# A transformer layer step with padded weight rows and padded token tiles

## The chip, the cores and the metric

The kernel runs on one core of a Trainium2 chip. The metric is the device time of one execution in microseconds (us); lower is better. A profile of one execution is at hand beside the times of three runs.

## The reference, cut to what matters

One layer of a decoder for 256 prompt tokens and 8 sample tokens, 264 tokens in all, with a model width of 2048. Everything is float32. Each line with `@` is a large weight matrix:

```
z  = rmsnorm(x) @ w_in                    # 2048 x 5128
x += concat(rg_lru(z), mlstm(z)) @ w_out  # recurrences of the two head groups
k, v = rmsnorm(mem) @ w_k, rmsnorm(mem) @ w_v    # 256 memory tokens
q  = rmsnorm(x) @ w_q
x += softmax(q k^T / sqrt(512)) v @ w_o   # 4 heads; samples use cached k, v
h  = silu(rmsnorm(x) @ w_gate) * (rmsnorm(x) @ w_up)   # 2048 -> 5632
x += h @ w_down
y  = rmsnorm(x)
```

## The kernel before

Tokens lie transposed: the 2048 features in 16 chunks of 128 partitions, the 264 tokens along the free dimension. A product with a weight matrix goes by *steps*: a step makes 128 output features for all tokens, from one piece of the weights of 128 partitions x 2048 columns (16 blocks of 128 x 128, 1 MB). There are 257 steps (16 of them, those of V, turn the operands round: the memory tokens are stationary and 512 columns of weights stream). The list `steps` holds them in order; the loop at line 1234 goes through it.

To keep float32's precision at the fast rate of the type float32r, each operand is split in two parts of float32r, high and low. `mm3` (line 179) multiplies one block by one chunk of tokens with three matmuls into the same bank: weights high by tokens high, high by low, low by high. Each of these matmuls comes with a load of its weight block (PEld in the profile), which runs while the matmul before it streams its tokens.

**Weights.** `load_piece` (line 142) issues a piece's DMA from SP's queue into one of 3 raw buffers of 2048 columns. SP's queue runs in the order in which it is written, two to three pieces ahead. `split_half` (line 150) splits a piece by halves of 1024 columns (8 blocks), one step ahead of the matmuls: ScalarE (ACT) copies the raw values to float32r in `wh`, VectorE (DVE) subtracts that from the raw ones into `wl`. Each of `wh` and `wl` has 4 buffers of 1024 columns, so two steps of two halves. `W` (line 169) gives a block's two parts to `mm3`. `split_gates` (line 506) does the same for the one step of the gates, whose 8 used columns allow both parts in one block.

**Tokens.** `Arr` (line 110) is an array of chunks, 4 chunks of 264 columns in one tile of the tag `B`, which has 26 slots; `HL` (line 124) is a pair of such arrays for high and low. The tag `B` serves everything else of that size too. A slot goes to the tile that asks next, so which slot a tile has follows from the order in which the program asks.

SBUF is laid out in the order in which tags are first asked for: the constants, then the tags `raw`, `B`, `wh`, `wl`, `t` and the smaller ones. Every tile begins at a multiple of 32 bytes.

**Start.** Lines 1211 to 1223 write out by hand the first loads on SP's queue: tokens in groups, the first piece in quarters among them, then pieces 1 and 2 with the third and fourth group of tokens. The first piece's halves are split in 4 and in 2 parts.

Other work (recurrences, norms, attention, the sample tokens' caches by GpSimd's queue) is put between the steps by `pump`, as far as the planned clocks of VectorE and ScalarE leave room.

Of the kernel before, what the change touches and what calls it, by code (L numbers as in the profile page):

```python
# [10 lines left out]
F32 = mybir.dt.float32  # L11
F32R = mybir.dt.float32r
I32 = mybir.dt.int32
AF = mybir.ActivationFunctionType
# [3 lines left out]
P = 128  # L18
# [4 lines left out]
N = T + NS  # L23
# [57 lines left out]
def layer_kernel(ctx: ExitStack, tc, xT, memT, vec, wrg, w_in, w_out, w_q, w_k, w_v, w_o,  # L81
# [3 lines left out]
    act, dve, pe = Engine(nc.scalar, price_act), Engine(nc.vector, price_dve), Engine(nc.tensor, price_pe)  # L85
    pool_e, sp = nc.gpsimd, nc.sync

    const = ctx.enter_context(tc.tile_pool(name="const", bufs=1))
    sb = ctx.enter_context(tc.tile_pool(name="sb", bufs=1))
# [2 lines left out]
    ctx.enter_context(tc.manual_schedule(engines={mybir.EngineType.SP}))  # L92

    uid = [0]

    def nm(s):
        uid[0] += 1
        return f"{s}_{uid[0]}"

    def B(shape, dt=F32):  # L100
        return sb.tile(shape, dt, tag="B", bufs=NB, name=nm("B"))

    def tmp(w=N, tag="t"):
        t = sb.tile([P, N], F32, tag=tag, bufs=NT if tag == "t" else NL, name=nm(tag))
        return t[:, :w]

    def ltmp(w=N):
        return tmp(w, "lt")

    class Arr:  # L110


# [2 lines left out]

        def tile(self, q):
            if q not in self.t:
                self.t[q] = B([P, min(4, self.nb), self.w], self.dt)
            return self.t[q]

        def __call__(self, c):
            return self.tile(c // 4)[:, c % 4, :]
# [14 lines left out]
    steps = []  # L137
    LD, LS = 3, 1

    raws, splits = {}, {}  # L140

    def load_piece(i):
        if i >= len(steps) or i in raws:
            return
        src, cols = steps[i][0], steps[i][1]
        r = sb.tile([P, 2048], F32, tag="raw", bufs=3, name=nm("raw"))
        sp.dma_start(r[:, :cols], src)
        raws[i] = r

    def split_half(i, h, parts=1):  # L150
        if i >= len(steps):
            return
        if steps[i][2] is pe_if:
            if h == 0:
                split_gates(i)
            return
        cols = steps[i][1]
        lo, hi = h * 1024, min(cols, (h + 1) * 1024)
        wh = sb.tile([P, 1024], F32R, tag="wh", bufs=4, name=nm("wh"))
        wl = sb.tile([P, 1024], F32R, tag="wl", bufs=4, name=nm("wl"))  # L160
        r = raws[i]
        n = (hi - lo) // parts
        with tc.high_priority():
            for o in range(0, hi - lo, n):
                st["split"] = act.activation(wh[:, o: o + n], r[:, lo + o: lo + o + n], AF.Copy)
                dve.tensor_sub(wl[:, o: o + n], r[:, lo + o: lo + o + n], wh[:, o: o + n])
        splits[i, h] = (wh, wl)

    class W:
        def __init__(self, i):  # L170
            self.i = i

        def __call__(self, c, w=P):
            per = 1024 // w
            wh, wl = splits[self.i, c // per]
            o = (c % per) * w
            return wh[:, o: o + w], wl[:, o: o + w]

    def mm3(ps, a, b, start, stop):
        ah, al = a  # L180
        bh, bl = b
        pe.matmul(ps, ah, bh, start=start, stop=False)
        pe.matmul(ps, ah, bl, start=False, stop=False)
        pe.matmul(ps, al, bh, start=False, stop=stop)

    st = {}
# [18 lines left out]
    def side(g, prio=0):  # L205
        x = Gen(g, prio)
        gens.append(x)
        gens.sort(key=lambda q: q.prio)
        return x
# [25 lines left out]
    def bank(tag="mm"):  # L235
        return psm.tile([P, 512], F32, tag=tag, bufs=4, name=nm(tag))

    warm_act = const.tile([P, 1], F32, name="warm_act")
    act.activation(warm_act, ones[:, 0:1], AF.Square)

    def warm(n, w=None):
# [263 lines left out]

    def split_gates(i):

        r = raws[i]
        for h in range(2):
            w = sb.tile([P, 8, P], F32R, tag="wh", bufs=4, name=nm("wh"))  # L510
            x = r[:, h * 1024: h * 1024 + 1024].rearrange("p (c m) -> p c m", m=P)
            with tc.high_priority():
                act.activation(w[:, :, 0:64], x[:, :, 0:64], AF.Copy)
                dve.tensor_sub(w[:, :, 64:128], x[:, :, 0:64], w[:, :, 0:64].bitcast(F32))
            splits[i, h] = w
# [303 lines left out]
    def proj(src, rhs, evac, cols=2048, n=N, need=()):  # L819

        def f(i):
            ps = bank()
            w = W(i)
            nch = cols // P
            for c in range(nch):
                mm3(ps[:, :n], w(c), rhs(c), c == 0, c == nch - 1)
            return ps
        steps.append((src, cols, f, evac, need))
# [191 lines left out]
    def evac_k(h, j):  # L1020
        def f(ps):
            if j == 0:
                kv["k", h] = HL(4, T)
            t = tmp(T)
            act.activation(t, ps[:, :T], AF.Copy)
            pool_e.dma_start(o_k[:, 4 * h + j, :], t)
            kh, kl = kv["k", h](j)
            act.activation(kh, ps[:, :T], AF.Copy)
            dve.tensor_sub(kl, ps[:, :T], kh.bitcast(F32))
            if j == 3:  # L1030
                st["att", h] = side(attend(h), 1)
        return f

    def pe_v(h, k4):
        def f(i):
            if k4 == 0:
                kv["vps"] = [bank(), bank()]
            w = W(i)
            for c in range(4):
                kc = k4 * 4 + c  # L1040
                mh, ml_ = rm(kc)
                wh, wl = w(c, 512)
                for tb in range(2):
                    ps = kv["vps"][tb]
                    s = slice(tb * P, tb * P + P)
                    pe.matmul(ps, mh[:, s], wh, start=(kc == 0), stop=False)
                    pe.matmul(ps, mh[:, s], wl, start=False, stop=False)
                    pe.matmul(ps, ml_[:, s], wh, start=False, stop=(kc == KC - 1))
            return kv["vps"]
        return f  # L1050

    def evac_vm(h):
        def f(vps):
            vv = B([P, 2, 512], F32R), B([P, 2, 512], F32R)
            kv["v", h] = vv
            vf = B([P, 2, 512])
            for tb in range(2):
                vh = vv[0][:, tb, :]
                act.activation(vh, vps[tb], AF.Copy)
                dve.tensor_sub(vv[1][:, tb, :], vps[tb], vh.bitcast(F32))  # L1060
                act.activation(vf[:, tb, :], vps[tb], AF.Copy)
                pool_e.dma_start(o_v[tb * P: tb * P + P, h * 512: h * 512 + 512], vf[:, tb, :])
            kv["vn"] = h + 1
        return f
# [57 lines left out]
    for h in range(H):  # L1122
        for j in range(4):
            proj(w_k[4 * h + j], rm, evac_k(h, j), n=T, need=("memg",))
        for k4 in range(4):
            steps.append((w_v[h, k4], 2048, pe_v(h, k4), evac_vm(h) if k4 == 3 else None, ()))

    def ro(c):
        return st["o"](c)
# [81 lines left out]
    def load_x(lo, hi):  # L1211
        sp.dma_start(xres[:, lo:hi, :], xT[:, lo:hi, :])

    r = sb.tile([P, 2048], F32, tag="raw", bufs=3, name=nm("raw"))
    raws[0] = r
    for h in range(4):
        if h < 2:
            load_x(2 * h, 2 * h + 2)
        sp.dma_start(r[:, h * 512: h * 512 + 512], w_in[0][:, h * 512: h * 512 + 512])
    for q in range(1, 4):  # L1220
        load_x(4 * q, 4 * q + 4)
        if q < 3:
            load_piece(q)

    with tc.high_priority():
        for c in range(KC):
            split(*xn(c), xres[:, c, :], V("g_mix", c))
            if c == 1:
                split_half(0, 0, 4)
            elif c == 3:  # L1230
                split_half(0, 1, 2)

    pend = []
    for i, (src, cols, pef, evf, need) in enumerate(steps):
        load_piece(i + LD - 1)
        if i == 5:
            finish(lambda: fn.done)
# [9 lines left out]
        now = pe.clock  # L1247
        dve.clock, act.clock = max(dve.clock, now), max(act.clock, now)
        split_half(i + LS, 0)
        if i + LS < len(steps) and steps[i + LS][1] > 1024:  # L1250
            split_half(i + LS, 1)
# [7 lines left out]
        if evf is not None:  # L1259
            pend.append((evf, ps))  # L1260
        load_piece(i + LD)
        pump(pe.clock + SLACK)
        if i == 24:
# [5 lines left out]
    for lo, hi in ((0, 1), (1, 2), (2, 4), (4, 6), (6, 8), (8, 10), (10, 12), (12, 14), (14, 16)):  # L1269
        for c in range(lo, hi):  # L1270
            e, r = (pool_e, rstd) if c in POOLC else (dve, fin["ps"][:, :N])
# [108 lines left out]
```

## Time and profile before

| | |
|---|---|
| median of 3 runs | 1575.6 us (1570.88 to 1576.71) |
| the profiled execution | 1576.51 us |
| its span, from the first to the last instruction | 1574.8 us |
| TensorE busy (PE) | 1556.5 us, 99% |
| VectorE (DVE), ScalarE (ACT) busy | 1051.4 us, 789.7 us |
| moved by DMA | 325.97 MB, mean 207 GB/s |
| mean granted TensorE clock | 0.991 |

In the profile, PE is TensorE's matmuls and PEld its weight loads; `mm<-B,wh` is a matmul into a bank `mm` from a token tile `B` and a weight tile `wh`. L60 is the line of a helper that issues every instruction of ACT, DVE and PE, so groups are told apart by tiles. "128x264" is partitions by columns of the streamed operand. A row of the timeline has its start in us, its length in us, the engine and the instruction; neighbours that are alike are merged (x2).

### The profile page before, as it was taken

Reading aid. Unit: us, or ns where it says so; the run is one execution under the profiler, and the core shown is the slowest. Engines: PE = TensorE matmul, PEld = TensorE weight load, DVE = VectorE, ACT = ScalarE, POOL = GpSimd, SP = SyncE. Lnnn points to the kernel's source line nnn. Section 1 sums busy time; section 2 is a strip of 40 time slices with the busy share of each in tenths; the row PEclk is TensorE's granted clock in tenths of the full one; section 3 lists DMA queues with packets and bytes.
Section 4 is the critical chain, followed back from the end, with each engine's and each line's share of the span. In section 5 each row is a group of like instructions: output and inputs, shape, how many; then the busy total and the mean of one; then the engine's idle time right before and its main releaser. Section 6 shows DMA issues by size and latency. Waiting matters only on the chain.

```text
span 1574.8 us, 29829 instructions
## 1 busy us (share of the span) xinstructions
PE 1556.5 (99%) x12340; PEld 1532.6 (97%) x12340; DVE 1051.4 (67%) x2021; ACT 789.7 (50%) x1252; POOL 109.6 (7%) x174
## 2 busy tenths in 40 slices
PE   9999999999999999999999999999999999999997
PEld 8999999999999889999999999999999999999997
DVE  7876877787699899956655555455555554555554
ACT  7465675565455656645444444333444433344463
POOL 0001210000124333200000000000000000000000
PEclk9999999999999999999999999999999999999998
DMA  8455875546689788745545555555455554555452
GB/s 304 161 174 172 294 269 205 178 145 245 248 321 346 302 305 319 251 161 178 187 164 185 188 180 175 181 188 186 174 179 186 187 181 172 184 188 184 156 179 99
DMA packets 55303, 325.97 MB, mean 207 GB/s; under 512 B 6688, under 2 KB 7120, under 8 KB 24448
## 3 DMA queue, kind: packets, MB, share of 16 engines
q1 hardware_dynamic: 39744, 270.68, 48.4%
q0 software_dynamic: 15136, 53.16, 9.4%
q8 instruction: 96, 1.57, 0.4%
q14 instruction: 39, 0.32, 0.1%
q10 hardware_dynamic: 288, 0.23, 0.1%
HBM read 312.78 MB, written 11.28 MB: 206 GB/s over the span
## 4 chain that ended last, share of the span: by engine, by line
PE 94%; DMA 2%; DVE 2%; ACT 1%; issue 1%; DVEq 0%; POOL 0%; SPq 0%; ACTq 0%
PE mm L60 89%; PE ax L60 4%; DVE B L60 1%; DMA o_sc<-B 1%; ACT B L60 1%; DMA raw<-w_in 1%; ACT wh L60 0%; DMA B<-scr 0%; DVE wl L60 0%; ACT L60 0%; DMA vecs<-vec 0%; DMA scr<-lt 0%; DVE t L60 0%; DVE dw L60 0%; ACT t L60 0%
## 5 line engine op out<-in xcount | busy, mean ns | idle before, releaser
L60 PE MATMUL mm<-B,wh 128*128 128x264 f32 (+1 forms) x7520 | 1379.0, 285 | 4.8 <-DVE B L60 3.0
L60 PEld LDWEIGHTS mm<-B,wh 128*128 128x128 f32 x7520 | 1168.4, 189 | 6.4 <-ACT cso L60 3.1
L60 PE MATMUL mm<-B,wl 128*128 128x264 f32 (+1 forms) x3744 | 1062.8, 284 | 0.6 <-DVE wl L60 0.6
L60 ACT ACTIVATE wh<-raw 128x1024 fp32r<-128x1024 f32 (+2 forms) x518 | 536.9, 1038 | 692.0 <-PE mm L60 574.6
L60 DVE TENSOR_TENSOR wl<-raw,wh 128x1024 fp32r<-128x1024 f32 (+2 forms) x516 | 619.0, 1201 | 356.7 <-ACT wh L60 350.0
L60 PEld LDWEIGHTS mm<-B,wl 128*128 128x128 f32 x3744 | 706.7, 189 | 1.1 <-DVE wl L60 1.0
L60 DVE TENSOR_TENSOR t<-mm,rstd 128x264 f32<-128x264 f32 x104 | 44.9, 432 | 60.2 <-PE mm L60 60.2
L60 PE MATMUL mm<-wh,B 128*128 128x512 f32 x256 | 82.3, 395 | 0.0
L60 DVE TENSOR_TENSOR xres<-xres,mm 128x264 f32<-128x264 f32 x80 | 34.2, 428 | 47.1 <-PE mm L60 47.1
L1272 POOL TENSOR_TENSOR B<-B,rstd 128x264 f32<-128x264 f32 x4 | 2.8, 743 | 864.9 <-ACT rstd L60 864.9
L60 PEld LDWEIGHTS mm<-wh,B 128*128 128x128 f32 x256 | 47.8, 189 | 9.8
L60 DVE SCALAR_TENSOR_TENSOR B<-B,dw 128x256 f32<-128x256 f32 x128 | 52.6, 465 | 2.3 <-ACT dw L60 2.3
L60 PE MATMUL mm<-wl,B 128*128 128x512 f32 x128 | 50.6, 395 | 0.0
L60 DVE SCALAR_TENSOR_TENSOR dw<-B,qsm,dw 128x256 f32<-128x256 f32 x96 | 47.9, 500 | 1.4 <-ACT dw L60 0.7
L60 PE MATMUL ax<-B,B 128*128 128x256 f32 (+3 forms) x288 | 48.2, 308 | 0.3 <-DVE B L60 0.3
L60 PEld LDWEIGHTS ax<-B,B 128*128 128x128 f32 x288 | 40.8, 189 | 4.0 <-issue 1.2
L977 POOL TENSOR_TENSOR ds<-dw,ds 128x256 fp32r<-128x256 f32 x32 | 35.4, 1107 | 115.3 <-ACT ds L60 115.2
L60 ACT ACTIVATE B<-xres,vecs 128x264 fp32r<-128x264 f32 (+1 forms) x64 | 31.1, 503 | 2.5 <-DMA xres<-xT 1.4
L60 ACT ACTIVATE t<-xres 128x264 f32<-128x264 f32 x60 | 23.9, 413 | 15.4 <-DVE xres L60 15.4
L60 PEld LDWEIGHTS mm<-wl,B 128*128 128x128 f32 x128 | 24.1, 188 | 5.0
L966 POOL DMA_DIRECT2D B<-kcT x32 | 17.5, 546 | 147.4 <-DVE B L60 127.0
L60 DVE TENSOR_TENSOR acc_x<-acc_x,t 128x264 f32<-128x264 f32 x59 | 25.2, 428 | 0.9 <-ACT t L60 0.5
(157 smaller groups left out, 740.0 us busy)
## 6 DMA issues: line engine op xcount, KB each, us to landing
raw<-w_gu SPq DMA_DIRECT2D x88, 1024.0 KB, 4.8
raw<-w_in SPq DMA_DIRECT2D x40, 1024.0 KB, 4.9
raw<-w_d SPq DMA_DIRECT2D x32, 1024.0 KB, 4.8
raw<-w_out SPq DMA_DIRECT2D x16, 1024.0 KB, 4.8
B<-kcT POOLq DMA_DIRECT2D x32, 512.0 KB, 6.1
raw<-w_q SPq DMA_DIRECT2D x16, 1024.0 KB, 5.0
B<-vcT POOLq DMA_DIRECT2D x32, 512.0 KB, 7.2
raw<-w_k SPq DMA_DIRECT2D x16, 1024.0 KB, 6.4
```

The source lines that it names most:

```text
L60: return f(*a, **k)
L966: pool_e.dma_start(kc, kcT[h, b])
L977: pool_e.tensor_sub(ws[:, 1], acc, ws[:, 0].bitcast(F32))
L1272: e.tensor_mul(st["y"](c), st["y"](c), r)
```

## The change

Five things change together; no arithmetic does.

- Every token tile of the tag `B` has 4 x 264 + 32 = 1088 columns. In arrays of 264 columns, tiles of odd number begin 32 columns (128 bytes) into theirs; others begin at 0.
- The two parts of a half piece share one tile `w` of 8 x 264 + 64 = 2176 columns, of which there are 4. From column 48 on it has 8 rows of 264 columns, one for each block: 128 columns of the high part and, right behind them, 128 of the low part; 8 columns are left unused. The gates' step uses the same rows.
- The steps of K and V (`wide`) keep contiguous parts: high in columns 0 to 1023 and low in 1056 to 2079 of such a tile.
- The raw buffers are halves of 1024 columns, 5 of them in place of 3 of 2048, and each piece is loaded by two DMAs, the first piece's quarters into its two halves.
- A small tile `pad` of 16 columns is the first in its pool, and the constant `warm_act` becomes a column of it. That takes 32 bytes from the constants and puts 64 ahead of `raw`, so that `raw`, `B` and `w` begin on a multiple of 256 bytes.

```diff
+    pad = sb.tile([P, 16], F32, tag="pad", bufs=1, name="pad")
...
+    BW = 4 * N + 32
+    WO, WW = 48, 8 * N + 64
...
         def tile(self, q):
             if q not in self.t:
-                self.t[q] = B([P, min(4, self.nb), self.w], self.dt)
+                t, o = B([P, BW], self.dt), 32 * (q % 2) if self.w == N else 0
+                self.t[q] = t[:, o: o + 4 * self.w].rearrange("p (c n) -> p c n", n=self.w)
             return self.t[q]
...
         src, cols = steps[i][0], steps[i][1]
-        r = sb.tile([P, 2048], F32, tag="raw", bufs=3, name=nm("raw"))
-        sp.dma_start(r[:, :cols], src)
-        raws[i] = r
+        raws[i] = []
+        for o in range(0, cols, 1024):
+            r = raw_half()
+            w = min(1024, cols - o)
+            sp.dma_start(r[:, :w], src[:, o: o + w])
+            raws[i].append(r)
+
+    def raw_half():
+        return sb.tile([P, 1024], F32, tag="raw", bufs=5, name=nm("raw"))
...
-        cols = steps[i][1]
-        lo, hi = h * 1024, min(cols, (h + 1) * 1024)
-        wh = sb.tile([P, 1024], F32R, tag="wh", bufs=4, name=nm("wh"))
-        wl = sb.tile([P, 1024], F32R, tag="wl", bufs=4, name=nm("wl"))
-        r = raws[i]
-        n = (hi - lo) // parts
+        nch = min(8, steps[i][1] // P - 8 * h)
+        w = sb.tile([P, WW], F32R, tag="w", bufs=4, name=nm("w"))
+        if i in wide:
+            wh, wl = w[:, 0: 1024], w[:, 1056: 2080]
+            with tc.high_priority():
+                act.activation(wh, raws[i][h], AF.Copy)
+                dve.tensor_sub(wl, raws[i][h], wh.bitcast(F32))
+            splits[i, h] = (wh, wl)
+            return
+        wh, wl = wrows(w, i)
+        r = raws[i][h].rearrange("p (c m) -> p c m", m=P)
+        n = nch // parts
         with tc.high_priority():
-            for o in range(0, hi - lo, n):
-                st["split"] = act.activation(wh[:, o: o + n], r[:, lo + o: lo + o + n], AF.Copy)
-                dve.tensor_sub(wl[:, o: o + n], r[:, lo + o: lo + o + n], wh[:, o: o + n])
+            for o in range(0, nch, n):
+                k = slice(o, o + n)
+                st["split"] = act.activation(wh[:, k], r[:, k], AF.Copy)
+                dve.tensor_sub(wl[:, k], r[:, k], wh[:, k].bitcast(F32))
         splits[i, h] = (wh, wl)
+
+    def wrows(w, i):
+        w = w[:, WO: WO + 8 * N].rearrange("p (c n) -> p c n", n=N)
+        return w[:, :, 0: P], w[:, :, P: 2 * P]
...
         def __call__(self, c, w=P):
+            if w == P and self.i not in wide:
+                wh, wl = splits[self.i, c // 8]
+                return wh[:, c % 8], wl[:, c % 8]
...
-            w = sb.tile([P, 8, P], F32R, tag="wh", bufs=4, name=nm("wh"))
-            x = r[:, h * 1024: h * 1024 + 1024].rearrange("p (c m) -> p c m", m=P)
+            w = wrows(sb.tile([P, WW], F32R, tag="w", bufs=4, name=nm("w")), i)[0]
+            x = raws[i][h].rearrange("p (c m) -> p c m", m=P)
```

More of the change, by code (lines that the diff above doesn't have):

```diff
@@ L138, in layer_kernel @@
     LD, LS = 3, 1
-    raws, splits = {}, {}
+    raws, splits, wide = {}, {}, set()
     def load_piece(i):
@@ L236, in bank @@
         return psm.tile([P, 512], F32, tag=tag, bufs=4, name=nm(tag))
-    warm_act = const.tile([P, 1], F32, name="warm_act")
+    warm_act = pad[:, 0:1]
     act.activation(warm_act, ones[:, 0:1], AF.Square)
@@ L506, in split_gates @@
     def split_gates(i):
-        r = raws[i]
         for h in range(2):
-            w = sb.tile([P, 8, P], F32R, tag="wh", bufs=4, name=nm("wh"))
-            x = r[:, h * 1024: h * 1024 + 1024].rearrange("p (c m) -> p c m", m=P)
+            w = wrows(sb.tile([P, WW], F32R, tag="w", bufs=4, name=nm("w")), i)[0]
+            x = raws[i][h].rearrange("p (c m) -> p c m", m=P)
             with tc.high_priority():
@@ L1124, in layer_kernel @@
             proj(w_k[4 * h + j], rm, evac_k(h, j), n=T, need=("memg",))
+            wide.add(len(steps) - 1)
         for k4 in range(4):
             steps.append((w_v[h, k4], 2048, pe_v(h, k4), evac_vm(h) if k4 == 3 else None, ()))
+            wide.add(len(steps) - 1)
     def ro(c):
@@ L1212, in load_x @@
         sp.dma_start(xres[:, lo:hi, :], xT[:, lo:hi, :])
-    r = sb.tile([P, 2048], F32, tag="raw", bufs=3, name=nm("raw"))
-    raws[0] = r
+    raws[0] = [raw_half(), raw_half()]
     for h in range(4):
@@ L1218, in layer_kernel @@
             load_x(2 * h, 2 * h + 2)
-        sp.dma_start(r[:, h * 512: h * 512 + 512], w_in[0][:, h * 512: h * 512 + 512])
+        sp.dma_start(raws[0][h // 2][:, h % 2 * 512: h % 2 * 512 + 512], w_in[0][:, h * 512: h * 512 + 512])
     for q in range(1, 4):
```

## The prediction

> **What bounds the kernel now.** I read the page first (engines, chain), then the groups by form, then two windows of the late stage, then the timeline of TensorE in one step of it.
>
> ```profile
> span 1574.8 us, 29829 instructions
> ...
> PE 1556.5 (99%) x12340; PEld 1532.6 (97%) x12340; DVE 1051.4 (67%) x2021; ACT 789.7 (50%) x1252; POOL 109.6 (7%) x174
> ...
> PE 94%; DMA 2%; DVE 2%; ACT 1%; issue 1%; DVEq 0%; POOL 0%; SPq 0%; ACTq 0%
> ```
> ```profile
> L60 PE MATMUL mm<-B,wh 128*128 128x264 f32 x7008 | 1286.0, 285 | 4.1 <-DVE B L60 3.0 <-ACT wh L60 1.1
> L60 PE MATMUL mm<-B,wl 128*128 128x264 f32 x3488 | 991.1, 284 | 0.6 <-DVE wl L60 0.6
> L60 PE MATMUL mm<-B,wh 128*128 128x256 f32 x512 | 93.1, 281 | 0.6 <-ACT B L60 0.5
> L60 PE MATMUL mm<-wh,B 128*128 128x512 f32 x256 | 82.3, 395 | 0.0
> L60 PE MATMUL mm<-B,wl 128*128 128x256 f32 x256 | 71.8, 280 | 0.0
> L60 PE MATMUL mm<-wl,B 128*128 128x512 f32 x128 | 50.6, 395 | 0.0
> ...
> L60 PE MATMUL ax<-B,wh 128*128 128x264 f32 x64 | 13.6, 313 | 1.7 <-ACT wh L60 1.7
> L60 PE MATMUL ax<-B,wl 128*128 128x264 f32 x32 | 9.0, 297 | 0.0
> ```
> ```profile
> 800.00:900.00 100.00, 100.00 (x830) 100.00 (x829) 57.21 (x79) 43.89 (x54) 0.00 (x0) 1.00 0.52 180
> 900.00:1000.00 100.00, 100.00 (x828) 100.00 (x828) 55.54 (x67) 40.80 (x48) 0.00 (x0) 1.00 0.51 179
> ```
>
> TensorE is 99% busy and carries 94% of the chain, and hardly a wait is left: its rows of 264 columns show 4.1, 0.6, 1.7 and 0.0 us of idle time before them. These four rows hold 7008 + 3488 + 64 + 32 = 10,592 matmuls of 264 columns. All but the gates' 32 come in threes (high·high, high·low, low·high), which I call a chunk: 3,520 chunks. In the windows the granted clock is 1.00 and 100 us hold 828 to 830 matmuls, one every 120.6 ns. The listed 285 ns of one matmul is its latency, since matmuls overlap. So the time changes almost only by the pace of these chunks: 1 ns a chunk is 3.5 us, and 0.5% of the time (7.9 us, about what a measurement of this kernel can tell from no change) is 2.2 ns a chunk.
>
> **Does that pace hang on addresses?** The timeline gives chunk by chunk what the windows average (wh x2 begins a chunk; a chunk lasts to the next such row):
>
> ```profile
> 1100.62 0.41 PE L60 MATMUL mm<-B,wh 128*128 128x264 f32 x2
> 1100.87 0.28 PE L60 MATMUL mm<-B,wl 128*128 128x264 f32 x1
> 1100.99 0.28 PE L60 MATMUL mm<-B,wh 128*128 128x264 f32 x1
> ```
> ```profile
> 1103.88 0.41 PE L60 MATMUL mm<-B,wh 128*128 128x264 f32 x2
> 1104.13 0.28 PE L60 MATMUL mm<-B,wl 128*128 128x264 f32 x1
> 1104.25 0.40 PE L60 MATMUL mm<-B,wh 128*128 128x264 f32 x2
> 1104.49 0.28 PE L60 MATMUL mm<-B,wl 128*128 128x264 f32 x1
> 1104.61 0.41 PE L60 MATMUL mm<-B,wh 128*128 128x264 f32 x2
> ...
> 1105.33 0.40 PE L60 MATMUL mm<-B,wh 128*128 128x264 f32 x2
> 1105.57 0.28 PE L60 MATMUL mm<-B,wl 128*128 128x264 f32 x1
> 1105.69 0.28 PE L60 MATMUL mm<-B,wh 128*128 128x264 f32 x1
> ```
>
> Chunks of one step last 0.37, 0.37, 0.36 and 0.36 us (371, 366, 357 and 354 ns in the records' whole nanoseconds). To sort them I put addresses beside the records, from the order in which tiles are asked for. A token tile of the kernel before is 4 x 264 x 4 = 4224 bytes, 128 modulo 256, and a chunk's row in it 1056 bytes, 32 modulo 256; weight blocks follow each other by 512 bytes, 0 modulo 256, and the 26 token tiles before them end on a multiple of 256 too. So, with "distance" for where a matmul's token row begins less where the weight block that is loaded meanwhile begins, modulo 256: it is 0 or 128 by the tile's slot, plus 32 for each chunk in the tile. Of the chunks from 300 us on, 2,834 have all records in a row; the first and the last begin here:
>
> ```profile
> 300.29 0.41 PE L60 MATMUL mm<-B,wh 128*128 128x264 f32 x2
> ...
> 1559.70 0.40 PE L60 MATMUL mm<-B,wh 128*128 128x264 f32 x2
> ```
>
> Their mean is 363.4 ns. Where high and low tokens have the same distance, the means are 361.3 (distance 0), 362.9 (32), 364.2 (64), 357.5 (96), 367.1 (128), 370.0 (160), 361.6 (192) and 366.4 (224), from 207 to 300 chunks each; the shortest mixed class that lasts is 354. So the pace does hang on something that the distance tracks, by up to 4%, though classes scatter by 2 to 4 ns inside.
>
> The Trainium skill ("TensorE: Matmul & The Clock Gate", section "Step-by-step: what each phase is for") says that TensorE has two independent SBUF read ports, so that loading the next weights takes nothing from the running matmul. By that rule the new addresses would be worth 0 and the sum would stay at the time before; the spread of 354 to 371 ns inside one step is hard to square with it.
>
> **The change, part by part.**
>
> Distances. Token tiles become 4352 bytes (17 x 256), and odd tiles begin 128 bytes in, so that row c lies at 32c modulo 256. A weight row becomes 1056 bytes, high at its start and low 512 bytes on, beginning 192 bytes into the tile: 192 + 32c for both. Token and weight pools begin alike modulo 256 (5 halves of 4096 and 26 tiles of 4352 lie between). So the first two matmuls of every chunk get distance -192 = 64, and the third, during which chunk c+1's block is loaded, 32. Before, a chunk of class 64 had 123.5 + 119.9 + 120.8 = 364.2 ns (300 chunks), and the third matmul of class 32 had 120.7. From above, then: 123.5 + 119.9 + 120.7 = 364.1 ns, 0.7 over the mean, +2.5 us. From below: that first matmul's 123.5 also follows one at distance 32, 3.1 ns over the other two's mean of 120.4; the step back from 64 to 32 has no row, and if it returns the 3.1 the chunk is 361.0, -2.4 x 3,520 = -8.4 us. I take the middle, 362.6: **-3 us**.
>
> The 1,152 matmuls of K and V (256 and 512 columns) alternate between distances 0 and 128 after as before: 0, with 1 ns either way (the spread of a class) 1.2 us up or down.
>
> Raw halves. Each step's load becomes two issues, and five half buffers hold 2.5 steps in place of 3.
>
> ```profile
> L60 ACT ACTIVATE wh<-raw x404: 614/1062/1090, 300.8 to 1499.9; 128x1024 fp32r<-128x1024 f32 x134, 128x512 fp32r<-128x512 f32 x1
> L60 DVE TENSOR_TENSOR wl<-raw,wh x403: 686/1226/1771, 299.0 to 1496.6; 128x1024 fp32r<-128x1024 f32 x134, 128x512 fp32r<-128x512 f32 x1
> L147 SPq DMA_DIRECT2D raw<-w_gu x88: 327/328/328, 771.5 to 1464.4; - x88
> ...
> L147 SPq DMA_DIRECT2D raw<-w_out x12: 327/328/328, 300.2 to 366.3; - x12
> ...
> DMA to landing us min/median/max: 4.2/4.8/9.6
> ```
> ```profile
> SPq L147 <- DVE wl L60: 872.5, 154, 18.2
> ```
>
> The seven rows of issues in these 1200 us, of which the first and the last stand here, count 202: as many more x 0.328 us = 66 us on SP's queue, which waits 872.5 us of the span for splits to free raw buffers. So there is room for them. The fifth half buffer back from a piece's second half is the first half of the piece two earlier; so it goes out about two steps (48 matmuls x 121 ns = 5.8 us each, 11.6 us) ahead of its own split, against a landing of 4.8 us, 9.6 at most, for the whole megabyte. Hidden: 0. If that cover goes: the longest landing, an issue and the two splits make 9.6 + 0.33 + 1.06 + 1.23 = 12.2 us, 0.6 too late.
>
> Start. The fourth group of tokens is queued behind piece 2's second half, which waits for the split of piece 0's first half:
>
> ```profile
> 7.15 0.33 SPq L1212 DMA_DIRECT2D xres<-xT  x1
> ```
> ```profile
> 8.52 2.02 DVE L60 TENSOR_TENSOR wl<-raw,wh 128x256 fp32r<-128x256 f32 x4
> ```
> ```profile
> 20.98 1.32 ACT L60 ACTIVATE B<-xres,vecs 128x264 fp32r<-128x264 f32 x3
> ```
>
> It goes out near 9.7 us (two of those four pieces are the half's) in place of 7.15 and is read at 20.98: 11 us of cover, 0 (up to 1 us).
>
> Splits in rows of 128. The gates' split already reads and writes strided rows, and the last part's half piece is contiguous:
>
> ```profile
> 54.32 0.69 DVE L60 TENSOR_TENSOR wh<-raw,wh 128x512 fp32r<-128x512 f32 x1 [0.79 <-ACT wh L60]
> ```
> ```profile
> 1485.97 0.69 DVE L60 TENSOR_TENSOR wl<-raw,wh 128x512 fp32r<-128x512 f32 x1 [0.17 <-ACT wh L60]
> ```
>
> Both take 0.69 us: 0. High and low now share a tile; should a first matmul have to wait for the low part too, that is one VectorE split (twice 0.69 for a half) later, a step ahead of use: 0. VectorE and ScalarE, 56% and 42% busy in the two windows together, bound nothing.
>
> Sum: 1576.5 (the profiled execution: its span and 1.7 around it; the median of the runs is 0.9 lower) - 3 = **1573 us**; this case's own range, with all bounds above, 1566 to 1581.
>
> **The rivals.**
>
> A steady distance settles lower (faster). Before, the distance moved by 32 each chunk and jumped by 128 between tiles; here one pattern repeats 3,520 times. If the two reads fall into step then, class 64 is no guide, and the pace of the best steady class is open: 357.5, -5.9 x 3,520 = -21 us, 1556. For it: in class 96 the chunk stays within 357 to 359 ns, whatever slots its tiles are in. Against it: by slots, no group of class 64 has a mean below 361.
>
> The stall goes nearly whole (faster still). If the 354 ns chunk is what is left when reads rarely meet: -9.4 x 3,520 = -33 us, 1543, and some ns less a chunk would reach 1532. For it: chunks of 354 recur every second step. Against it: they are a mixed class. The skill's same page ("Back-to-back issue gap") gives N/2.4 + 2.5 ns, by estimate 112.5 ns for 264 columns and 1485 us in all; no chunk here ran at that.
>
> The wrong distance is fixed everywhere (slower). Now good and bad classes average out; one pattern in every chunk gives that up. If the place that counts is the block in use or an absolute address, so that 64 stands where 160 stood, 370.0: +6.6 x 3,520 = +23 us, 1600; it decides from 365.6 ns a chunk.
>
> Raw halves arrive late (slower): 0.6 us, as above, in half of the 32 steps of K and V (768 + 384 matmuls), which share the DMA engines with other loads: +10 us, 1586. Against it: the median landing is half of the longest.
>
> **How the numbers follow.** Forecast 0.34; settles lower 0.28; stall gone 0.18; wrong distance 0.15; late halves 0.05. Faster by over 0.5%: 0.46; within: 0.34; slower: 0.20. The likeliest gives 1573. The range runs to 1532, half of the stall-gone case, and to 1592, short of most of the wrong-distance case: about 2 in 10 are left out.
>
> **What would show it.** Matmuls in 800 to 1000 us: 829 x 363.4 / 362.6 = 831 per 100 us by the forecast, 843 if it settles lower, 851 with the stall gone, 814 with the wrong distance. Every chunk of a step should last the same. The splits stay at 1.06 and 1.23 us, and neither DMA nor SP should end a wait of TensorE. A pace outside 361 to 364 ns makes the prediction wrong whatever the time.

## The result, and the profile after

The changed kernel takes 1558.54 us (1555.69 to 1559.8, 4 runs) against 1576.15 us before (4 runs): a ratio of 0.9901, 95% interval [0.9887, 0.9915]. A second time, beside other kernels, it was 1558.5 us against 1575.09 us (14 runs), 0.9895 [0.988, 0.991]. So it is 1.0% faster, by 17 us where the forecast of 1573 us meant 3, and inside the range. The profiled execution took 1555.69 us.

Its page, the same lines as of the kernel before:

```profile
span 1554.0 us, 30608 instructions
...
PE 1537.1 (99%) x12340; PEld 1513.7 (97%) x12340; DVE 1049.7 (68%) x2021; ACT 786.9 (51%) x1252; POOL 108.2 (7%) x174
...
PE 97%; ACT 1%; DVE 1%; DMA 0%; issue 0%; DVEq 0%; SPq 0%; ACTq 0%
```

The number of matmuls is the same, VectorE and ScalarE work as long as before, and TensorE is still 99% busy, in a span that is 20.8 us shorter. So its matmuls follow each other faster. One window over the late stage shows by how much; first the kernel before, then the changed one (after the window's bounds and length come busy time and count of each engine, then the granted clock):

```profile
800.00:1400.00 600.00, 600.00 (x4960) 600.00 (x4959) 326.35 (x391) 244.64 (x280) 0.00 (x0) 1.00 0.52 181
```
```profile
800.00:1400.00 600.00, 600.00 (x5014) 600.00 (x5013) 328.72 (x385) 244.00 (x282) 0.00 (x0) 1.00 0.55 184
```

5014 in place of 4960 matmuls in 600 us at the full clock, 836 per 100 us: one every 119.7 ns in place of 121.0. Sorted as in the prediction, from 300 us on, a chunk of the changed kernel takes **359.3 ns** (2,799 chunks with all records in a row) in place of 363.4. All but 16 of them (the last chunks of the last steps, which have 12 blocks) have the distances worked out beforehand: 64, 64 and 32. By position they take 120.3, 119.8 and 119.2 ns.

The early part gains more than that. The rows from 200 to 300 us, before and after:

```profile
200.00:300.00 100.00, 100.00 (x801) 99.79 (x800) 79.50 (x197) 61.48 (x117) 4.78 (x9) 0.97 0.61 219
```
```profile
200.00:300.00 100.00, 100.00 (x840) 99.97 (x839) 77.98 (x181) 57.95 (x106) 4.22 (x8) 1.00 0.64 215
```

39 matmuls more, where the pace accounts for 9: the granted clock was 0.97 and is 1.00. In the records of the clock the kernel before has three stretches at half clock before 300 us, from 47, 126 and 238 us on, of 6.83 us each; the changed kernel has two of 3.41 us, from 47 and 125 on. In such a stretch matmuls come half as fast (24 from 240 to 245 us before, 43 from 230 to 235), so it costs half its length: 10.2 us before, 3.4 after.

So the 20.8 us of the two spans are: 3,520 chunks x 4.1 ns = 14.4 us; stretches at half clock 6.8 us; less 1.1 us for K (768 matmuls of 256 columns, 117.9 to 119.3 ns) and 0.2 us for V (384 of 512 columns, 231.8 to 232.2 ns); 0.9 us are left, shorter waits among them.

### The profile page after: what moved, and what is told of

Same layout as the page of the kernel before. It is cut to its first block, busy times and chain, and to the rows that moved or that the text cites. A ratio compares the mean times of both kernels' runs of the same rounds, so it can differ in the third digit from the quotient of the medians.

```text
span 1554.0 us, 30608 instructions
## 1 busy us (share of the span) xinstructions
PE 1537.1 (99%) x12340; PEld 1513.7 (97%) x12340; DVE 1049.7 (68%) x2021; ACT 786.9 (51%) x1252; POOL 108.2 (7%) x174
## 4 chain that ended last, share of the span: by engine, by line
PE 97%; ACT 1%; DVE 1%; DMA 0%; issue 0%; DVEq 0%; SPq 0%; ACTq 0%
PE mm L60 92%; PE ax L60 5%; DVE B L60 1%; ACT B L60 1%; DMA raw<-w_in 0%; ACT w L60 0%; ACT L60 0%; DVE w L60 0%; DVE c L60 0%; DVEq L1387 0%; DVE xres L60 0%; ACT t L60 0%; ACT rstd L60 0%; SPq L1243 0%; ACT c L60 0%
## 5 line engine op out<-in xcount | busy, mean ns | idle before, releaser
L60 PE MATMUL mm<-B,w 128*128 128x264 f32 (+1 forms) x11264 | 1369.5, 283 | 3.7 <-DVE B L60 2.2
L60 PEld LDWEIGHTS mm<-B,w 128*128 128x128 f32 x11264 | 1358.6, 188 | 5.3 <-ACT cso L60 2.2
L60 ACT ACTIVATE w<-raw 128x1024 fp32r<-128x1024 f32 (+2 forms) x518 | 537.0, 1038 | 655.1 <-PE mm L60 452.0
L60 DVE TENSOR_TENSOR w<-raw,w 128x1024 fp32r<-128x1024 f32 (+2 forms) x518 | 620.0, 1198 | 363.4 <-ACT w L60 362.4
L60 PE MATMUL mm<-w,B 128*128 128x512 f32 x384 | 92.8, 395 | 0.0
L60 PEld LDWEIGHTS mm<-w,B 128*128 128x128 f32 x384 | 70.5, 188 | 15.3
L60 ACT ACTIVATE dw<-B,qsm 128x256 f32<-128x256 f32 x32 | 16.3, 509 | 19.6 <-DVE B L60 9.5
L60 DVE SCALAR_TENSOR_TENSOR B<-xres,vecs,B 128x264 fp32r<-128x264 f32 x48 | 22.6, 487 | 4.5 <-ACT B L60 4.4
L60 ACT ACTIVATE t<-t 128x264 f32<-128x264 f32 (+1 forms) x61 | 24.8, 406 | 1.3 <-DVE t L60 1.2
L60 ACT ACTIVATE t<-B,B 128x128 f32<-128x128 f32 x64 | 21.6, 390 | 6.1 <-DMA B<-scr 6.1
```

The source lines that it names most:

```text
L60: return f(*a, **k)
```

## The experiments

**Undo one thing: the place of the weight rows.** Only `WO`, the column at which the weight rows begin, is changed; tokens stay where they are. 8 columns are 32 bytes, so eight values take the distance once around 256 bytes (`WO` = 48 is the changed kernel). Each value has one run. The first four:

```diff
-    WO, WW = 48, 8 * N + 64
+    WO, WW = 40, 8 * N + 64
```

> The weight rows begin 160 bytes into their tile in place of 192: distances 96, 96, 64 in place of 64, 64, 32. Read in the windows from 800 to 1400 us, where the changed kernel has 837.5 matmuls per 100 us (359.3 ns a chunk). If the class means of the kernel before carry over (the best class was 96, 357.5 ns): 842. If only steadiness counts, or only the tokens' own addresses: 837 to 838, as with 64.

> The weight rows begin 96 bytes in: distances 160, 160, 128. If the class means of before carry over (the worst class, 370.0 ns): 813 matmuls per 100 us between 800 and 1400 us, and a time near 1590 us. If only steadiness or the tokens' own addresses count: 837 to 838 and about 1558 us.

> The weight rows begin 64 bytes in: distances 192, 192, 160. By the class means of before (361.6 ns): 832 matmuls per 100 us between 800 and 1400 us. By steadiness or the tokens' own addresses alone: 837 to 838.

> The weight rows begin 224 bytes in: distances 32, 32, 0. By the class means of before (362.9 ns): 829 matmuls per 100 us between 800 and 1400 us. By steadiness or the tokens' own addresses alone: 837 to 838.

The late windows, in the same order, one fence for each kernel:

```profile
800.00:1400.00 600.00, 600.00 (x4991) 600.00 (x4990) 327.69 (x385) 243.14 (x281) 0.00 (x0) 1.00 0.55 182
```
```profile
800.00:1400.00 600.00, 600.00 (x4901) 600.00 (x4900) 322.12 (x388) 240.16 (x276) 0.00 (x0) 1.00 0.53 179
```
```profile
800.00:1400.00 600.00, 600.00 (x4945) 600.00 (x4945) 324.94 (x382) 241.77 (x280) 0.00 (x0) 1.00 0.54 181
```
```profile
800.00:1400.00 600.00, 600.00 (x4900) 600.00 (x4900) 321.34 (x377) 240.57 (x277) 0.00 (x0) 1.00 0.54 179
```

Per 100 us that is 832 (distance 96), 817 (160), 824 (192) and 817 (32) against 836 (the 837.5 of the expectations is from windows of 100 us, where the matmuls that straddle an edge weigh more). Moving nothing but the weights takes part of the gain away at 96 (1561.91 us) and all of it at 192, 32 and 160; with 160 the kernel takes 1588.32 us, slower than before (1575.76 us on the same chip). That ends the theories that steadiness alone, or the tokens' own addresses alone, made the gain. The class means of before do badly too: they put 96 ahead of 64 and expected 829 for 32.

The other three:

> The weight rows begin with their tile: distances 0, 0, 224. Five distances have been seen by now: 359.3 ns a chunk (64), 361.1 (96), 364.1 (192), 366.8 (32), 368.1 (160). By the class means of the kernel before (361.3 for 0) 833 matmuls per 100 us between 800 and 1400 us. If a chunk is smooth in the distance, 0 lies beside 32 and is as slow: 820.

> The weight rows begin 128 bytes in: distances 128, 128, 96. By the class means of the kernel before (367.1): 820 matmuls per 100 us between 800 and 1400 us. If smooth between 96 (361.1) and 160 (368.1): 825.

> The weight rows begin 32 bytes in: distances 224, 224, 192. By the class means of the kernel before (366.4): 821 matmuls per 100 us between 800 and 1400 us. If smooth between 192 (364.1) and 32 (366.8): 823.

```profile
800.00:1400.00 600.00, 600.00 (x4945) 600.00 (x4945) 324.35 (x382) 242.97 (x280) 0.00 (x0) 1.00 0.53 181
```
```profile
800.00:1400.00 600.00, 600.00 (x4990) 600.00 (x4989) 328.28 (x396) 244.06 (x282) 0.00 (x0) 1.00 0.54 182
```
```profile
800.00:1400.00 600.00, 600.00 (x4961) 600.00 (x4960) 326.11 (x384) 242.60 (x280) 0.00 (x0) 1.00 0.54 182
```

824, 832 and 827. Neither rule held: 0 is better than its neighbour 32, and 128 better than between 96 and 160. The whole scan, by the records from 300 us on (time: one execution each, 64 the median of four):

| distance of the first two matmuls | ns a chunk | by position | us |
|---|---|---|---|
| 64 (the changed kernel) | 359.3 | 120.3, 119.8, 119.2 | 1558.5 |
| 96 | 361.1 | 120.9, 116.4, 123.9 | 1561.9 |
| 128 | 362.4 | 121.2, 119.1, 122.1 | 1574.2 |
| 224 | 362.6 | 120.8, 120.9, 120.9 | 1569.5 |
| 192 | 364.1 | 121.2, 119.3, 123.6 | 1575.6 |
| 0 | 364.3 | 122.5, 118.6, 123.3 | 1574.8 |
| 32 | 366.8 | 123.2, 122.7, 121.0 | 1580.3 |
| 160 | 368.1 | 122.5, 122.1, 123.5 | 1588.3 |

The mean of the eight is 363.6 ns, and the kernel before, which runs through all eight, has 363.4. So one distance kept is worth nothing by itself; what gains is which one is kept. 128 has nearly the chunk of 96 but takes 12 us longer: 5.1 us are half clock (17.1 us of such stretches against 6.8), and before 300 us, which the table leaves out, its chunks average 370 ns against 362.

Six of these eight means mix several paces, though. Take the chunks stream by stream, a *stream* being chunks that follow each other with no other matmul and no other order of matmuls in between. By the records from 200 us on, nearly every stream settles on one pace and keeps it to its end, whether it has 30 chunks or the 1,900 from about 800 us on, which make up two thirds of each mean. At 64 all long streams take 359.1 to 359.6 ns a chunk and at 96 360.8 to 361.6. At 128 some take 361 and others 374; at 192 it is 360.8, 364.1 or 374, at 160 367.5 or 369.7. So the distance limits which paces can come, and something else picks one for each stream. That 64 is best holds for every long stream; the order of rows that lie a few ns apart hangs on that pick.

**Shift both.** The tile ahead of the raw buffers grows, so tokens and weights move together by 96 bytes:

```diff
-    pad = sb.tile([P, 16], F32, tag="pad", bufs=1, name="pad")
+    pad = sb.tile([P, 40], F32, tag="pad", bufs=1, name="pad")
```

> The small tile ahead of the raw buffers has 40 columns in place of 16, so tokens and weights both begin 96 bytes later modulo 256 and every distance stays 64, 64, 32. If the distance alone counts: 837 to 838 matmuls per 100 us between 800 and 1400 us, as in the changed kernel. If absolute addresses count (tokens at 96 + 32c in place of 32c), the pace leaves that by more than 2 per 100 us, or the chunks swap their order in the row of eight.

```profile
800.00:1400.00 600.00, 600.00 (x5014) 600.00 (x5013) 329.13 (x388) 244.51 (x282) 0.00 (x0) 1.00 0.55 184
```

The same 5014, 359.3 ns a chunk (120.2, 119.8, 119.2) and 1557.61 us. Only the order of quicker and slower chunks in the row (358 to 361 ns, repeating every four) moved. So at this distance the pace hangs on where tokens lie against weights, not on where both lie modulo 256; that the new pools begin on a multiple of 256 bytes does nothing for it.

**The tokens' part alone.** The kernel before with padded token tiles and raw halves, weights as they were:

```diff
-                self.t[q] = B([P, min(4, self.nb), self.w], self.dt)
+                t, o = B([P, BW], self.dt), 32 * (q % 2) if self.w == N else 0
+                self.t[q] = t[:, o: o + 4 * self.w].rearrange("p (c n) -> p c n", n=self.w)
```

> The kernel before with raw halves and padded token tiles, weights contiguous as before: high and low tokens of a chunk now always have the same distance, but it runs through all eight values from chunk to chunk. If a chunk costs what its distance costs: the mean of the eight values of the scan, 363.6 ns, so within 0.3% of the kernel before once the half-clock stretches are taken out. If the agreement of high and low tokens is what helps: near 359 ns and 14 us faster.

```profile
800.00:1400.00 600.00, 600.00 (x4968) 600.00 (x4967) 326.19 (x384) 245.64 (x281) 0.00 (x0) 1.00 0.54 182
```

362.6 ns a chunk: 0.8 under before, not the 4.1 of the whole change. So the agreement of high and low tokens brings little of the quicker chunk, and the raw halves do no harm. Its time fell more than that, 0.9954 [0.9938, 0.997] or 7 to 9 us, close to half of the whole change's 17, where chunks give 2.8 us and V's matmuls (227.8 ns in place of 231.8) 1.5, and K's (119.7 in place of 117.9) take 1.4; where the rest comes from stays open. Its eight classes run from 357.0 (96) and 357.5 (0) to 367.5 (160) and 370.7 (224), unlike the scan. Six lie within 4 ns of those of before, but 128 has 358.5 where it had 367.1, and 224 has 370.7 where it had 366.4: a class has no fixed price in mixed layouts either.

**Another distance for the second matmul.** The low part goes to the front of its row:

```diff
-        return w[:, :, 0: P], w[:, :, P: 2 * P]
+        return w[:, :, N - P: N], w[:, :, 0: P]
-    WO, WW = 48, 8 * N + 64
+    WO, WW = 40, 8 * N + 64
```

> In each weight row the low part comes first and the high part begins 544 bytes behind it (8 unused columns lie between), and the rows begin 160 bytes in: the high parts stay where they were, so the distances of the first and the third matmul stay 64 and 32, and that of the second becomes 96 in place of 64. By position the scan had for the second matmul 116.4 ns at 96 and 119.8 at 64. If the three positions add up: 355.9 ns a chunk, 845 matmuls per 100 us between 800 and 1400 us, some 12 us under the changed kernel. If only the whole pattern counts: another of the values that the scan had, 359 to 368 ns, so no faster than the changed kernel.

```profile
800.00:1400.00 600.00, 600.00 (x4988) 600.00 (x4989) 328.47 (x396) 244.68 (x282) 0.00 (x0) 1.00 0.54 183
```

363.9 ns a chunk, by position 117.9, 121.2, 124.8, and 1.0006 [0.9996, 1.0016] of the time before. Only the second matmul's distance changed, yet it became slower, the first faster, and the third, whose distance stayed, 5.6 ns slower.

This mean too hides two paces. Two windows of 80 us, both at the full clock:

```profile
715.00:795.00 80.00, 80.00 (x647) 80.00 (x647) 49.08 (x69) 38.27 (x54) 0.00 (x0) 1.00 0.56 183
```
```profile
900.00:980.00 80.00, 80.00 (x667) 80.00 (x666) 45.12 (x55) 33.42 (x42) 0.00 (x0) 1.00 0.55 185
```

By the records the 235 chunks from 712 us on take 372.0 ns (123.1, 122.2, 126.7), the 1,898 from 807 us on 360.8 (115.8, 120.8, 124.2), and the last 174 371.7 again, all at the distances 64, 96 and 32. Fifteen chunks of the first of these streams have the very slots and buffers of chunks of the second; they take 371.9 ns there and 360.8 here. So positions don't add up in either pace (355.9 was forecast), and the layout alone doesn't set the price: a stream keeps the pace that it has fallen into. What makes it fall into one or the other no run isolates, and as this kernel was profiled once, whether it would fall the same way again is not shown.

**Both kernels again, for the half clock.**

> The changed kernel once more, beside the others on one chip: 0.99 of the kernel before, 359.3 ns a chunk. It shows whether the stretches at half clock in the first 300 us (two of 3.4 us in its first profile, three of 6.8 us in that of the kernel before) belong to the kernel or to the run: if to the kernel, the same two again.

> The kernel before once more, for its profile: 363.4 ns a chunk. If the half-clock stretches belong to the run, others than the three of 6.8 us of its first profile; if they belong to the kernel, the same three.

The rows from 200 to 300 us, of the kernel before and of the changed one, each run again:

```profile
200.00:300.00 100.00, 100.00 (x800) 99.78 (x800) 78.94 (x197) 61.50 (x117) 4.77 (x9) 0.97 0.60 218
```
```profile
200.00:300.00 100.00, 100.00 (x838) 99.89 (x837) 78.04 (x181) 58.24 (x106) 4.23 (x8) 1.00 0.64 220
```

The chunks are those of the first profiles to 0.1 ns. The stretches are nearly so: 3.4, 6.8 and 6.8 us near the same three places before, 3.4 and 3.4 us after. Their places stay with the kernel, their lengths vary with the run. The pace doesn't settle the places: the kernel with the common shift has two, from 48 and 232 us on. In the kernel before and in the changed one, the first stretch (from 47.25 and 46.59 us on) begins inside a wait of TensorE:

```profile
48.17 0.78 PE L60 MATMUL mm<-B,wh 128*128 128x264 f32 x2 [3.03 <-DVE B L60]
```
```profile
47.04 3.15 PE L60 MATMUL mm<-B,w 128*128 128x264 f32 x13 [2.18 <-DVE B L60]
```

The wait is shorter in the changed kernel (2.18 us after 3.03), but that doesn't settle the stretch's length: the kernel before, run again, has the same wait of 3.03 us and a stretch of 3.4. The one from 238 us on has no wait ahead of it. What lies there, in the kernel before, are matmuls of a single column, which count as busy while they stream next to nothing:

```profile
235.50 2.12 PE L60 MATMUL ax<-ones,B 128*128 128x1 f32 x18
```

The changed kernel has 24 of them in a row (2.74 us from 229.15 us on) and no stretch there; the one with the common shift has them (from 229.84) and the stretch. So they are a candidate for what sets it off, and not all of it. Mean clocks of single runs go from 0.991 to 0.995 before (14 runs, mean 0.993) and from 0.992 to 0.996 after (8 runs, mean 0.994). So, by estimate from these means, a typical run keeps about 0.001 x 1575 = 1.6 us of the profiles' 6.8, which would explain why the medians differ by 16.6 to 17.6 us and the profiles by 20.8.

## Why the prediction was right, and where it was not

**What bounds the kernel:** right. 1 ns a chunk was to be worth 3.5 us. From the changed kernel to the one with distance 32: 7.5 ns x 3,520 = 26.4 us, less 1.7 for a shorter stretch at half clock, against 24.6 us between the spans (1578.6 and 1554.0); to the one with 160: 31.0 + 3.4 against 32.6 (1586.6).

**Distances:** right, 64, 64 and 32, worked out from the code; the scan and the common shift show that they count, and the two paces at one set of distances that they are not all that counts.

**The price of the chunk:** this step failed. The text put 123.5 + 119.9 + 120.7 from above and 361.0 from below, and took 362.6; the chunk takes 359.3, below both bounds and outside the 361 to 364 that the text gave as the sign of being wrong (838 matmuls per 100 us between 800 and 1000 us where it had 831). Position by position: the second came out (119.8), the third lay between its bounds (119.2 of 117.6 to 120.7), the first did not: 120.3 in place of 123.5, 3.2 ns x 3,520 = 11.3 us. I had taken the 123.5 for the price of a step from distance 32 to 64, which every chunk of the new layout takes as well. But in a class 64 chunk of before that step came out of three matmuls at 32, and none stepped back. Class means were prices inside their own surroundings, and were taken for a price of the distance, where a stream can settle on more than one pace at one distance: before they put 96 first and 32 ahead of 64; kept throughout, 64 is first and 32 next to last. Hence 1573 us and its own range, 1566 to 1581, were too slow. That the stated range held the result is due to the rivals' share of it and not to the sum.

**Edits costed at nothing:** right. The halves' issues take 0.33 us each as before, land in 3.6 us (9.0 at most), and no TensorE wait ends on them; the fourth group of tokens goes out at 9.11 us (9.7 expected):

```profile
L159 SPq DMA_DIRECT2D raw<-w_gu x176: 327/328/328, 759.5 to 1447.6; - x176
...
DMA to landing us min/median/max: 2.6/3.6/9.0
```
```profile
9.11 0.43 SPq L1243 DMA_DIRECT2D xres<-xT  x1
```

**The rivals.** "A steady distance settles lower" came nearest by its number (1556 us) and is right in that streams do settle on a pace, but settling is not what gains: the eight steady distances are as a set no better than the mixture, and a stream can settle high (374 ns). "The wrong distance" did not happen here and does at 160 and 32. The stall did not go whole: no steady distance came under 359. Every chunk of a step was to last the same; they stay within 358 to 360 ns by their place in the row.

**The half clock** had no term in the sum. It is 6.8 us of the profiled difference and, by the estimate above, 1.6 of a typical one.

By the Trainium skill ("TensorE: Matmul & The Clock Gate", section "Step-by-step: what each phase is for") loading the next weights takes nothing from the running matmul. Here it does, or something that looks the same, and the measurement decides: with tokens in place, moving only the weights changes three matmuls from 359.3 to 368.1 ns. What does that, why the best pattern is 64, 64, 32, and what picks a stream's pace, no run here shows.

## What to carry to other kernels

Where TensorE never waits and still falls short of its rate, look at where the streamed rows lie against the weights that are loaded meanwhile; a padded layout that keeps that distance constant makes it a knob, and the knob has to be scanned on the chip, since here the eight settings lie 2.5% apart and their mean is what the unpadded layout had anyway. Look at the pace stream by stream before you take a mean: here one layout has two paces 3% apart. Prices read from a mixed trace hold for their own surroundings: take them as a spread, not as a forecast for a pattern that the trace doesn't contain.

## What the runs showed of the hardware that was not expected

- The pace of matmuls of 264 columns repeats to 0.1 ns a chunk between runs of one layout, and a common shift of 96 bytes leaves it alone, while a shift of 32 bytes of one operand against the other changes it by up to 7.5 ns a chunk.
- At one set of distances and the full clock, an unbroken stream of chunks keeps one of several paces, 360.8 or 372 ns with 64, 96 and 32, for up to 685 us; chunks at the same addresses have either.
- Stretches at half clock of 3.4 or 6.8 us turn up at places that stay with a kernel (from 47, 126 and 238 us on before), the last of them though PE was busy for all of the 60 us from 178 to 238 us by the records, 2.12 us of it with matmuls of one column; in the scan, with nothing but the weights moved, there are one (distance 32) to four (128, 160, 192, 0) of them. Within a run their starts lie whole multiples of 3.413 us apart (before: 23 from 47.25 to 125.76 us, 56 from 47.25 to 238.40). What sets the last off stays open.
